# A two-layer encoder trunk: pooling groups and attention heads in turns, two heads projected ahead of the decay, the last norm multiplied early

## The chip, the cores and the metric

The kernel runs on one core of a Trainium2 chip. The metric is the device time of one execution in microseconds; the time before is the median of three runs. Engines are named as the profile names them: TensorE (PE, with its weight loads as PEld), VectorE (DVE), ScalarE (ACT), GpSimd (POOL) and the DMA queue of SyncE (SP).

## The reference

The input x has 512 tokens of 1024 channels in float32. There are two layers, each a token mixer and a feed-forward block, both with a root-mean-square norm ahead of them and a residual behind, and a final norm.

```python
# layer 0: q, k, v and u from one projection of 1024 -> 2048
a_out = diff_attention(q, k, v)      # 4 heads: softmax(q1 k1) - lam * softmax(q2 k2), times v, norm per head
b_out = pool_mixer(u)                # 4 groups of 128 channels: trailing mean over 2, 4, 8, 16 tokens - u, times a 128x128 matrix
x = x + concat(a_out, b_out) @ ab_w_out
x = x + relu(rmsnorm(x) @ w1)**2 @ w2
# layer 1: gated linear attention, 4 heads
q, k, v, g, gk = split(h @ w_in)
log_a = log_sigmoid(gk @ w_gk_up + b_gk) / 16       # the decay, summed up along the tokens of a chunk
o = chunked_linear_attention(q, k, v, log_a)
x = x + (rmsnorm_per_head(o) * silu(g)) @ w_out
x = x + relu(rmsnorm(x) @ w1)**2 @ w2
return rmsnorm(x) * norm_final
```

## The kernel before

Activations lie with the channels on the partitions, 128 at a time, and 512 tokens along the free axis. Every large matmul is done in three passes: weights and activations are each split into a high and a low part (`split_w` at L127 on ScalarE and L128 on VectorE for weights, `split` and `split_scaled` for activations), and high times high, high times low and low times high are added up in PSUM. `proj_T` (L149 to L151) makes one block of 128 output channels: 8 slices of the 1024 inputs, three matmuls each, 24 in all. `proj_tok` (L173 to L175) does the value projections for all four token tiles at once, 96 matmuls on four banks. Weights come in loads of 1 MB (L116) on the SP queue, two blocks a load.

Buffers come from pools with a tag each. The tag `row` has 54 buffers of 512 columns and serves nearly everything (`row`, `row8`, `row16` and `tmp2` are one function; outside the feed-forward blocks every second `tmp` comes from it too). The tag `tmp` has 4, the PSUM tags `mm` (projections) and `ax` (everything else) have 4 banks each. Raw weights and some other stages lie in parts of one large tile (`wraw`), among them a ring of three for the sums of the pooling groups (`row_u`).

The order on each engine is fixed ahead of time by the tile framework's planner. It takes, for each engine, the ready instruction that stands first in the program; `soon(n)`, a high priority, moves an instruction ahead by n places, and `tc.issue_after(i)` holds instructions of an engine behind the instruction i. So TensorE takes later projections when earlier work isn't ready.

Layer 0. The heads' scores and softmax come first (the loop that ends at L392), with the projections of the value and of later stages between. Then `attend(h)` for each of four heads: the value product L372 on TensorE, a square L375, a scaled copy L377, sums over the head (`col_sums`, L203 to L206), a reciprocal root in Ln, Exp and three VectorE steps (L210 to L212), a product L378 and the split L187, L188 into `cat[h]`. The transposes of the last softmax (L354, L356) stand before `attend` of the last head. After all heads come the four pooling groups, windows 16, 8, 4, 2: a projection, its eviction L409, one to four shifted sums L415, the remainder L418 to L421 into a `row` buffer, the product L423 and the split L181, L182 into `cat[4 + i]`. `add_out` then makes the output projection from `cat`; its first two blocks take the slices in order with that of head 3 kept for last (`late`).

Layer 1. Head 0's query and key are projected and evicted (L690, L691), then the decay of all four heads is worked out (L695 to L714: matmul, Abs, Exp, a minimum L700, then Ln under another activation table, a difference L713 and a scan L714). Two calls of `project()` follow in the program (two projections each, evicted by L732 and L735 with `soon()`), and then weights(0), values1(0), weights(1), `project()`, weights(2), values1(1), weights(3), the four `outputs`, the gates and `add_out`. `weights(h)` begins with L747 and L753.

The last feed-forward block works in four quarters c of seven products n each. `gather` (L576) adds a product to the accumulator `acc[t][nh]`: token tile t of four, half nh of two. The last product of the last quarter is done for one token tile after the other, and the final norm follows: squares with their sum (L629), a reciprocal root, and for each half one VectorE step that multiplies by the root and the gain (L637) and a store (L639).

Of the kernel before, what the change touches and what calls it, by code (L numbers as in the profile page):

```python
# [16 lines left out]
P = 128  # L17
S = 512
# [17 lines left out]
def trunk(ctx: ExitStack, tc: tile.TileContext, xT, par, lvl, lam4, wqk0, wu0, wv0, poolw, wo0,  # L36
# [141 lines left out]
    def split_scaled(src, col, tiles=None):  # L178

        ah, al = tiles or act_tiles()  # L180
        A.activation(ah, src, AF.Copy, scale=col)  # L181
        V.scalar_tensor_tensor(out=al, in0=src, scalar=col, in1=ah.bitcast(F32), op0=ALU.mult, op1=ALU.subtract)  # L182
        return ah, al
# [184 lines left out]
    def attend(h):  # L368

        po = PS("ax")  # L370
        for kb in range(NT):
            PE.matmul(po[:, kb * P:], v[kb][:, h * P:(h + 1) * P], pTs[h][kb][:, kb * P:], start=kb == 0,  # L372
                      stop=kb == NT - 1)
        q = tmp()
        A.activation(q, po, AF.Square)  # L375
        o = tmp2()
        A.activation(o, po, AF.Copy, scale=sub8)  # L377
        V.tensor_tensor(o, o, rsqrt(tmp(), col_sums(q, EPS), 1.0 / P), ALU.mult)  # L378
        cat[h] = split(o, (row16(dt=F32R), row16(dt=F32R)))

    pend = []
    for h in range(NH):
# [7 lines left out]
        if h == 1:  # L390
            with tc.issue_after(first_sum):
                values()  # L392
    for h in range(NH - 1):
        attend(h)
    for p in pend:
        transposes(*p)
    attend(NH - 1)


    pw = tmp2().rearrange("p (g c) -> p g c", g=4)  # L400
    nc.sync.dma_start(pw, poolw)
    st = Stream(wu0)
    for i, g in enumerate((3, 2, 1, 0)):
        w = POOL_W[g]
        ps = proj_T(st.next(), act)
        u = row_u()
        G.memset(u[:, 0:16], 0.0)
        with soon():
            V.tensor_tensor(u[:, 16:], ps, rb, ALU.mult)  # L409
        s, step, us = u, 1, [row_u(), row_u()]  # L410
        while step < w:
            s2 = us[0]
            us.reverse()
            G.memset(s2[:, 0:16], 0.0)
            V.tensor_tensor(s2[:, 16:], s[:, 16:], s[:, 16 - step:16 + S - step], ALU.add)  # L415
            s, step = s2, 2 * step
        r = tmp2()
        V.scalar_tensor_tensor(out=r[:, 16:], in0=s[:, 32:], scalar=1.0 / w, in1=u[:, 32:], op0=ALU.mult,  # L418
                               op1=ALU.subtract)
        V.tensor_tensor(r[:, 0:16], s[:, 16:32], prm[:, C_ICNT + 16 * g:C_ICNT + 16 * (g + 1)], ALU.mult)  # L420
        V.tensor_tensor(r[:, 0:16], r[:, 0:16], u[:, 16:32], ALU.subtract)  # L421
        psy = PS("ax")
        PE.matmul(psy, pw[:, g, :], r, start=True, stop=True)  # L423
        cat[NH + i] = split_scaled(psy, prm[:, C_PSC + g:C_PSC + g + 1], (row16(dt=F32R), row16(dt=F32R)))

    def add_out(arr, src, col, late):

# [39 lines left out]
    def ffn(w1, w2, act, nrm, col):  # L467
# [8 lines left out]
        if final:  # L476
            xb = xall.rearrange("p f (t d) -> p f t d", d=P)
            acc = [[xb[:, 4 * nh:4 * nh + 4, t, :] for nh in range(2)] for t in range(NT)]
            gb = [row8() for _ in range(2)]

        def halves():
            return row().rearrange("p (j n) -> p j n", j=2)

        for c in range(4):
# [85 lines left out]
            def gather(t, nh, ps, first=False):  # L570
                with soon():
                    if first and c == 0 and not final:
                        acc[t][nh] = row8()
                        A.activation(acc[t][nh], ps, AF.Copy)
                    else:
                        V.tensor_tensor(acc[t][nh], acc[t][nh], shaped(ps), ALU.add)  # L576

            def shaped(ps):
                return ps.rearrange("p (f d) -> p f d", d=P) if final else ps

            w = [prep(0), prep(1)]
            plan = ((X, True, 0, 0), (Y, True, 0, 0), (X, False, 0, 1), (Zs, True, 2, 1), (X, False, 2, 1),
                    (Zs, False, 0, 1))
            for n, (ps, first, t0, nh) in enumerate(plan):
                if n + 2 < 7:
                    w.append(prep(n + 2))
                product(n, w[n], ps, first)
                for t in range(2):
                    gather(t0 + t, nh, ps[t], n in (0, 2, 3))
            if c == 3 and not final:  # L590
                constants()
            if c < 3:
# [31 lines left out]
                finish(f, pst[f])  # L624
            return nxt, n

        def squares(t, nh, ss):
            q = tmp()
            A.activation(q.rearrange("p (f d) -> p f d", d=P), acc[t][nh], AF.Square, accum_out=ss[:, nh:nh + 1])  # L629

        def finish(t, ss):
            v = small(1)
            V.scalar_tensor_tensor(out=v, in0=ss[:, 0:1], scalar=EPS * D, in1=ss[:, 1:2], op0=ALU.add, op1=ALU.add)
            r = rsqrt(small(1), v, 1.0 / D)
            for nh in range(2):
                o = row8()
                V.scalar_tensor_tensor(out=o.rearrange("p (f d) -> p f d", d=P), in0=acc[t][nh], scalar=r,  # L637
                                       in1=gb[nh].rearrange("p (f d) -> p f d", d=P), op0=ALU.mult, op1=ALU.mult)
                nc.sync.dma_start(out[t * P:(t + 1) * P, nh * S:(nh + 1) * S], o)  # L639

        ss = [small(2) for _ in range(NT)]
        for t in range(2):
            product(6, w[6], X, False, (t,))
            gather(2 + t, 0, X[t])
            if t == 0:
                for u in range(2):
                    squares(u, 0, ss[u])
                    squares(u, 1, ss[u])
                    finish(u, ss[u])
                    squares(2 + u, 1, ss[2 + u])  # L650
            squares(2 + t, 0, ss[2 + t])
            finish(2 + t, ss[2 + t])

    act, nrm = add_out(wo0, cat, C_FFN0, NH - 1)

# [33 lines left out]
    with soon():  # L689
        V.scalar_tensor_tensor(out=qT0, in0=psq0[0], scalar=float(P) ** -0.5, in1=rb, op0=ALU.mult, op1=ALU.mult)  # L690
        evicted = V.tensor_tensor(kT0, psq0[1], rb, ALU.mult).ins  # L691
    es, ms, bs = [], [], []
    for h in range(NH):
        psu = PS("ax")
        PE.matmul(psu, wu[0:96, h * P:(h + 1) * P], gkl[0:96, :], start=True, stop=True)  # L695
        bcol = prm[:, C_BGK + h:C_BGK + h + 1]
        e, m = tmp(), tmp2()
        A.activation(e, psu, AF.Abs, bias=bcol)
        last = A.activation(e, e, AF.Exp, scale=-1.0)
        V.tensor_scalar(out=m, in0=psu, scalar1=bcol, scalar2=0.0, op0=ALU.add, op1=ALU.min)  # L700
        es.append(e)
        ms.append(m)
    with tc.issue_after(last.ins):
        last = A.preload_act_table_set("natural_log")
    with tc.issue_after(last.ins):
# [15 lines left out]
    def expo(out, src):  # L721
        with tc.issue_after(exps):
            last_exp[0] = A.activation(out, src, AF.Exp, scale=GT).ins

    qks = [(qT0, kT0)]

    def project():

        ps = proj_T(st.next(), act)
        qT, kT = row8(), row8()  # L730
        with soon():
            V.scalar_tensor_tensor(out=qT, in0=ps, scalar=float(P) ** -0.5, in1=rb, op0=ALU.mult, op1=ALU.mult)  # L732
        ps = proj_T(st.next(), act)
        with soon():
            V.tensor_tensor(kT, ps, rb, ALU.mult)  # L735
        qks.append((qT, kT))

    def weights(h):

# [119 lines left out]
            ot.append(o)  # L859


    project()
    project()
    weights(0)
    values1(0)
    weights(1)
# [112 lines left out]
```

## Time and profile before

| | us |
|---|---|
| median of three runs | 1107.49 (1107.05 to 1108.73) |
| the profiled execution | 1106.55 |
| its span, first to last instruction | 1104.8 |
| TensorE busy | 1073.0 (97%) |
| VectorE busy | 826.9 (75%) |
| ScalarE busy | 538.3 (49%) |
| mean granted clock of TensorE | 0.990 |

A busy share is that of the span; weight loads overlap the matmuls. The chain of waits that ended last lies on TensorE for 91% of the span, on VectorE for 4% and on ScalarE for 3%. The granted clock is given as a share of 2.4 GHz, so the lower of its two levels, 1.2 GHz, is 0.50.

### The profile page before, as it was taken

The page shows a single profiled execution, that of the slowest core. Times are in us where ns is not written, and L with a number is a line of the kernel's source. Part 1 is how long each engine was busy: PE and PEld are TensorE (multiplying, and loading weights), DVE is VectorE, ACT ScalarE, POOL GpSimd, SP SyncE. Part 2 cuts the span into 40 slices and gives each one's busy share as a digit, 9 for nine tenths or more (in the row PEclk, how much of TensorE's full clock was granted, in tenths as well). Part 3 has the DMA queues.
Part 4 walks back from the last instruction along what each step waited for, and adds up shares of the span by engine and source line. Part 5 has one row for each costly group of instructions (what it writes and reads, how often), then busy time and mean ns, then how long its engine had stood idle before and what let it go on. Part 6 is the DMA issues. An engine that isn't in the chain of part 4 may idle for free.

```text
span 1104.8 us, 12896 instructions
## 1 busy us (share of the span) xinstructions
PE 1073.0 (97%) x4968; PEld 863.6 (78%) x4968; DVE 826.9 (75%) x1234; ACT 538.3 (49%) x890; POOL 2.3 (0%) x20
## 2 busy tenths in 40 slices
PE   7999979999999999999989999999999999999996
PEld 5676648888888888888877778788888888888885
DVE  6847667696497597598878877865696696696696
ACT  6444525455454354454555456844553453453453
POOL 0000000000000000000000000000000000000000
PEclk9999979999999999999999999999999999999999
DMA  6222213214304304203222121433205206206102
GB/s 238 88 89 91 91 72 133 77 39 157 120 28 168 127 11 188 79 17 115 77 77 77 39 77 39 152 114 115 96 1 212 93 1 228 77 3 226 39 1 77
DMA packets 17917, 103.52 MB, mean 94 GB/s; under 512 B 2016, under 2 KB 3040, under 8 KB 6208
## 3 DMA queue, kind: packets, MB, share of 16 engines
q1 hardware_dynamic: 17712, 102.67, 25.8%
q8 instruction: 39, 0.64, 0.2%
q14 instruction: 22, 0.18, 0.1%
q10 hardware_dynamic: 144, 0.03, 0.0%
HBM read 100.59 MB, written 2.10 MB: 93 GB/s over the span
## 4 chain that ended last, share of the span: by engine, by line
PE 91%; DVE 4%; ACT 3%; issue 1%; DMA 1%; SPq 0%; DVEq 0%
PE psmm L149 14%; PE psmm L150 14%; PE psmm L151 14%; PE psmm L568 6%; PE psmm L567 6%; PE psmm L566 6%; PE psax L150 3%; PE psax L151 3%; PE psax L149 3%; PE psax L567 3%; PE psax L568 3%; PE psax L566 3%; PE psmm L173 2%; PE psmm L174 2%; PE psmm L175 2%; PE psax L326 1%
## 5 line engine op out<-in xcount | busy, mean ns | idle before, releaser
L127 ACT ACTIVATE wh<-wraw 128x1024 fp32r<-128x1024 f32 x230 | 243.5, 1061 | 402.6 <-PE psmm L150 161.1
L128 DVE TENSOR_TENSOR wl<-wraw,wh 128x1024 fp32r<-128x1024 f32 x230 | 280.8, 1222 | 70.9 <-ACT wh L127 69.9
L149 PE MATMUL psmm<-row,wh 128*128 128x512 f32 x736 | 289.4, 394 | 15.3 <-DVE wraw L409 7.2
L150 PE MATMUL psmm<-row,wh 128*128 128x512 f32 x736 | 290.7, 395 | 0.0
L151 PE MATMUL psmm<-row,wl 128*128 128x512 f32 x736 | 290.1, 394 | 0.6 <-DVE wl L128 0.6
L149 PEld LDWEIGHTS psmm<-row,wh 128*128 128x128 f32 x736 | 138.5, 189 | 47.8 <-DVE wraw L409 7.8
L151 PEld LDWEIGHTS psmm<-row,wl 128*128 128x128 f32 x736 | 138.8, 189 | 31.9 <-issue 2.6
L150 PEld LDWEIGHTS psmm<-row,wh 128*128 128x128 f32 x736 | 138.8, 189 | 31.0 <-issue 2.6
L566 PE MATMUL psmm<-wh,row 128*128 128x512 f32 x320 | 124.6, 389 | 0.0
L568 PE MATMUL psmm<-wl,row 128*128 128x512 f32 x320 | 124.6, 389 | 0.0
L567 PE MATMUL psmm<-wh,row 128*128 128x512 f32 x320 | 124.5, 389 | 0.0
L541 DVE TENSOR_TENSOR wraw<-wraw 128x1024 f32<-128x1024 f32 x64 | 77.4, 1222 | 0.3
L493 DVE TENSOR_TENSOR row<-row,row 128x512 fp32r<-128x512 f32 x112 | 75.2, 686 | 0.3 <-ACT row L492 0.3
L568 PEld LDWEIGHTS psmm<-wl,row 128*128 128x128 f32 x320 | 60.1, 188 | 12.4
L566 PEld LDWEIGHTS psmm<-wh,row 128*128 128x128 f32 x320 | 60.1, 188 | 12.4
L567 PEld LDWEIGHTS psmm<-wh,row 128*128 128x128 f32 x320 | 60.1, 188 | 12.4
L492 ACT ACTIVATE row<-row 128x512 fp32r<-128x512 f32 x112 | 65.7, 617 | 5.3 <-DVE row L519 5.3
L507 DVE SCALAR_TENSOR_TENSOR tmp<-psmm,rb 128x512 f32<-128x512 f32 x48 | 33.0, 688 | 45.7 <-PE psmm L151 45.7
L512 ACT ACTIVATE row<-tmp 128x256 f32<-128x256 f32 x128 | 45.8, 406 | 11.0 <-DVE tmp L507 10.7
L151 PE MATMUL psax<-row,wl 128*128 128x512 f32 x128 | 49.8, 389 | 0.0
L568 PE MATMUL psax<-wl,row 128*128 128x512 f32 x128 | 49.8, 389 | 0.0
L150 PE MATMUL psax<-row,wh 128*128 128x512 f32 x128 | 49.8, 389 | 0.0
(233 smaller groups left out, 1315.4 us busy)
## 6 DMA issues: line engine op xcount, KB each, us to landing
wraw<-in_w1a SPq DMA_DIRECT2D x16, 1024.0 KB, 4.8
wraw<-in_w2a SPq DMA_DIRECT2D x16, 1024.0 KB, 4.8
wraw<-in_w1b SPq DMA_DIRECT2D x16, 1024.0 KB, 4.8
wraw<-in_w2b SPq DMA_DIRECT2D x16, 1024.0 KB, 4.8
wraw<-in_wo SPq DMA_DIRECT2D x8, 1024.0 KB, 4.8
wraw<-in_wqk SPq DMA_DIRECT2D x7, 1024.0 KB, 4.8
wraw<-in_wv SPq DMA_DIRECT2D x6, 1024.0 KB, 4.7
wraw<-in_wg SPq DMA_DIRECT2D x4, 1024.0 KB, 4.8
```

Of the source, the lines that this page charges most:

```text
L127: ended["hi"] = A.activation(hi, src, AF.Copy).ins
L128: ended["lo"] = V.tensor_tensor(lo, src, hi.bitcast(F32), ALU.subtract).ins
L149: PE.matmul(ps, wh, ah, start=first, stop=False)
L150: PE.matmul(ps, wh, al, start=False, stop=False)
L151: ended["mm"] = PE.matmul(ps, wl, ah, start=False, stop=last).ins
L492: A.activation(hi, src, AF.Copy)
L493: V.tensor_tensor(lo, src, hi.bitcast(F32), ALU.subtract)
L512: A.activation(raw[name][:, j, :], r[:, th * 256:th * 256 + 256], AF.Square)
L541: V.tensor_tensor(out[k], in0[k], in1[k], ALU.subtract)
L566: PE.matmul(ps[t], hi, wh[:, cs], start=f, stop=False, skip_group_check=True)
L567: PE.matmul(ps[t], lo, wh[:, cs], start=False, stop=False, skip_group_check=True)
L568: PE.matmul(ps[t], hi, wl[:, cs], start=False, stop=l, skip_group_check=True)
```

## The change

Three edits. First, the loop over pooling groups becomes a function `pooled(i, g)`, and the program calls pooled(0), attend(0), pooled(1), attend(1), pooled(2), attend(2), the last transposes, pooled(3), attend(3). The load of the pooling matrices stays ahead of all of it. Second, `project()` and its first two calls move ahead of the decay, and the decay's first loop is put under `soon(150)`. Third, in the last quarter of the last feed-forward block, when products 1 and 4 are gathered, two quarters of the output are final: `early` takes their squares and multiplies them with the gain at once (`zs`). In the tail `finish(t)` then does one VectorE step for the other half, and ScalarE scales the early half by the root in place; both are stored. The order of the tail changes: the gather of token tile 2 comes ahead of the finish of tiles 0 and 1.

```diff
-    for h in range(NH - 1):
-        attend(h)
-    for p in pend:
-        transposes(*p)
-    attend(NH - 1)
...
-    for i, g in enumerate((3, 2, 1, 0)):
+
+    def pooled(i, g):
...
+    for h in range(NH - 1):
+        pooled(h, 3 - h)
+        attend(h)
+    for p in pend:
+        transposes(*p)
+    pooled(3, 0)
+    attend(NH - 1)
...
+            ss, zs = [small(2) for _ in range(NT)], {}
...
+            def squares(t, nh):
+                q = tmp()
+                A.activation(blocks(q), acc[t][nh], AF.Square, accum_out=ss[t][:, nh:nh + 1])
+
+            def early(t, nh):
+
+                squares(t, nh)
+                zs[t] = row8()
+                V.tensor_tensor(blocks(zs[t]), acc[t][nh], blocks(gb[nh]), ALU.mult)
...
                     gather(t0 + t, nh, ps[t], n in (0, 2, 3))
+                    if final and c == 3 and n in (1, 4):
+                        early(t0 + t, nh)
...
-            for nh in range(2):
-                o = row8()
-                V.scalar_tensor_tensor(out=o.rearrange("p (f d) -> p f d", d=P), in0=acc[t][nh], scalar=r,
-                                       in1=gb[nh].rearrange("p (f d) -> p f d", d=P), op0=ALU.mult, op1=ALU.mult)
-                nc.sync.dma_start(out[t * P:(t + 1) * P, nh * S:(nh + 1) * S], o)
...
+            nh = 1 if t < 2 else 0
+            o = row8()
+            V.scalar_tensor_tensor(out=blocks(o), in0=acc[t][nh], scalar=r, in1=blocks(gb[nh]), op0=ALU.mult,
+                                   op1=ALU.mult)
+            nc.sync.dma_start(out[t * P:(t + 1) * P, nh * S:(nh + 1) * S], o)
+            A.activation(zs[t], zs[t], AF.Copy, scale=r)
+            nc.sync.dma_start(out[t * P:(t + 1) * P, (1 - nh) * S:(2 - nh) * S], zs[t])
+
+        product(6, w[6], X, False, (0,))
+        gather(2, 0, X[0])
         for t in range(2):
...
+            squares(t, 1)
+            finish(t)
+        product(6, w[6], X, False, (1,))
+        squares(2, 0)
+        finish(2)
+        with soon():
+            gather(3, 0, X[1])
+            squares(3, 0)
+            finish(3)
...
+    qks = [(qT0, kT0)]
+
+    def project():
+
+        ps = proj_T(st.next(), act)
+        qT, kT = row8(), row8()
+        with soon():
+            V.scalar_tensor_tensor(out=qT, in0=ps, scalar=float(P) ** -0.5, in1=rb, op0=ALU.mult, op1=ALU.mult)
+        ps = proj_T(st.next(), act)
+        with soon():
+            V.tensor_tensor(kT, ps, rb, ALU.mult)
+        qks.append((qT, kT))
+
+    project()
+    project()
     es, ms, bs = [], [], []
     for h in range(NH):
...
+        with soon(150):
+            psu = PS("ax")
...
-    project()
-    project()
     weights(0)
```

## Rows read from the trace of the kernel before

**Rows 1.** Waits of TensorE: engine, line, releaser, us, times, longest.
```profile
PE psmm L149 <- DVE wraw L409: 7.2, 1, 7.2
```

**Rows 2.** GLA stage in order of time: start us, us, engine, line, operation, tiles.
```profile
546.35 0.39 PE L151 MATMUL psmm<-row,wl 128*128 128x512 f32 x1
...
556.73 0.63 ACT L699 ACTIVATE row<-row 128x512 f32<-128x512 f32 x1
...
565.12 2.33 DVE L714 TENSOR_TENSOR_SCAN row<-row,row 128x512 f32<-128x512 f32 x2
567.37 0.67 DVE L732 SCALAR_TENSOR_TENSOR row<-psmm,rb 128x512 f32<-128x512 f32 x1
...
568.09 0.80 PE L173 MATMUL psmm<-wh,row 128*128 128x512 f32 x1 [2.95 <-DVE row L732]
...
570.94 0.68 DVE L753 TENSOR_TENSOR tmp<-row 128x512 f32<-128x512 f32 x1
...
619.79 0.68 DVE L732 SCALAR_TENSOR_TENSOR row<-psmm,rb 128x512 f32<-128x512 f32 x1
```

**Rows 3.** Stretches: length, busy PE, PEld, DVE, ACT, POOL, then PEclk, DMA, GB/s.
```profile
134.80:148.15 13.35, 3.46 (x8) 1.61 (x8) 7.77 (x14) 4.34 (x8) 0.00 (x0) 0.61 0.48 177
148.15:151.40 3.25, 3.25 (x5) 1.50 (x5) 2.06 (x3) 0.69 (x1) 0.44 (x4) 0.52 0.00 0
568.10:571.20 3.10, 3.10 (x8) 2.50 (x9) 3.10 (x6) 0.00 (x0) 0.00 (x0) 0.51 0.00 0
668.80:721.70 52.90, 51.56 (x281) 43.54 (x280) 42.25 (x67) 40.84 (x57) 0.00 (x0) 1.00 0.29 100
1060.00:1087.00 27.00, 27.00 (x121) 22.37 (x120) 23.67 (x30) 14.28 (x18) 0.00 (x0) 1.00 0.00 1
```

**Rows 4.** The tail in order of time.
```profile
1087.35 0.69 DVE L576 TENSOR_TENSOR x<-x,psax 128x512 f32<-128x512 f32 x1 [0.26 <-PE psax L568]
...
1090.08 0.75 DVE L637 SCALAR_TENSOR_TENSOR row<-x,sm,row 128x512 f32<-128x512 f32 x1
...
1095.08 0.39 PE L568 MATMUL psmm<-wl,row 128*128 128x512 f32 x1
...
1096.00 0.68 DVE L576 TENSOR_TENSOR x<-x,psmm 128x512 f32<-128x512 f32 x1
...
1099.55 1.41 DVE L637 SCALAR_TENSOR_TENSOR row<-x,sm,row 128x512 f32<-128x512 f32 x2
1100.33 1.09 SPq L639 DMA_DIRECT2D out<-row  x2
```

**Rows 5.** Heads and pooling groups in order of time.
```profile
109.38 2.32 PE L372 MATMUL psax<-row,wraw 128*128 128x512 f32 x8
111.73 0.60 ACT L375 ACTIVATE tmp<-psax 128x512 f32<-128x512 f32 x1 [0.74 <-PE psax L372]
111.97 0.75 DVE L347 SCALAR_TENSOR_TENSOR wraw<-wraw,sm 128x512 f32<-128x512 f32 x1
...
119.96 0.69 DVE L188 TENSOR_TENSOR row<-row,row 128x512 fp32r<-128x512 f32 x1 [0.70 <-ACT row L187]
...
145.79 0.69 DVE L188 TENSOR_TENSOR row<-row,row 128x512 fp32r<-128x512 f32 x1 [0.69 <-ACT row L187]
146.40 0.67 DVE L418 SCALAR_TENSOR_TENSOR row<-wraw 128x496 f32<-128x496 f32 x1
...
147.40 0.69 DVE L409 TENSOR_TENSOR wraw<-psmm,rb 128x512 f32<-128x512 f32 x1
...
153.15 1.07 PE L423 MATMUL psax<-row,row 128*128 128x512 f32 x2
```

**Rows 6.** Costliest groups of the page: xcount, busy us, mean ns, idle before.
```profile
L128 DVE TENSOR_TENSOR wl<-wraw,wh 128x1024 fp32r<-128x1024 f32 x230 | 280.8, 1222 | 70.9 <-ACT wh L127 69.9
```

**Rows 7.** Groups of TensorE from 104.9 to 165.7.
```profile
L151 PE MATMUL psmm<-row,wl 128*128 128x512 f32 x44 | 18.4, 422 | 0.0
```

**Rows 8.** Groups of TensorE from 568 to 595.
```profile
L173 PE MATMUL psmm<-wh,row 128*128 128x512 f32 x26 | 11.3, 434 | 3.0 <-DVE row L732 3.0
```

More of the change, by code (lines that the diff above doesn't have):

```diff
@@ L575, in gather, with blocks @@
                     else:
-                        V.tensor_tensor(acc[t][nh], acc[t][nh], shaped(ps), ALU.add)
-            def shaped(ps):
+                        V.tensor_tensor(acc[t][nh], acc[t][nh], blocks(ps), ALU.add)
+            def blocks(ps):
                 return ps.rearrange("p (f d) -> p f d", d=P) if final else ps
+            def squares(t, nh):
[5 more added lines that the diff above has]
+                V.tensor_tensor(blocks(zs[t]), acc[t][nh], blocks(gb[nh]), ALU.mult)
             w = [prep(0), prep(1)]
@@ L625, in ffn, with finish @@
             return nxt, n
[L627 to L631, printed above, removed]
+        def finish(t):
             v = small(1)
-            V.scalar_tensor_tensor(out=v, in0=ss[:, 0:1], scalar=EPS * D, in1=ss[:, 1:2], op0=ALU.add, op1=ALU.add)
+            V.scalar_tensor_tensor(out=v, in0=ss[t][:, 0:1], scalar=EPS * D, in1=ss[t][:, 1:2], op0=ALU.add, op1=ALU.add)
             r = rsqrt(small(1), v, 1.0 / D)
-            for nh in range(2):
-                o = row8()
-                V.scalar_tensor_tensor(out=o.rearrange("p (f d) -> p f d", d=P), in0=acc[t][nh], scalar=r,
-                                       in1=gb[nh].rearrange("p (f d) -> p f d", d=P), op0=ALU.mult, op1=ALU.mult)
-                nc.sync.dma_start(out[t * P:(t + 1) * P, nh * S:(nh + 1) * S], o)
-        ss = [small(2) for _ in range(NT)]
-        for t in range(2):
[L643 to L652, printed above, removed]
+            nh = 1 if t < 2 else 0
[7 more added lines that the diff above has]
+        gather(2, 0, X[0])
+        for t in range(2):
+            squares(t, 1)
[7 more added lines that the diff above has]
+            finish(3)
     act, nrm = add_out(wo0, cat, C_FFN0, NH - 1)
@@ L691, in trunk @@
         evicted = V.tensor_tensor(kT0, psq0[1], rb, ALU.mult).ins
+    qks = [(qT0, kT0)]
[10 more added lines that the diff above has]
+    project()
     es, ms, bs = [], [], []
     for h in range(NH):
[L694 to L702, printed above, removed]
+        with soon(150):
+            psu = PS("ax")
+            PE.matmul(psu, wu[0:96, h * P:(h + 1) * P], gkl[0:96, :], start=True, stop=True)
+            bcol = prm[:, C_BGK + h:C_BGK + h + 1]
+            e, m = tmp(), tmp2()
+            A.activation(e, psu, AF.Abs, bias=bcol)
+            last = A.activation(e, e, AF.Exp, scale=-1.0)
+            V.tensor_scalar(out=m, in0=psu, scalar1=bcol, scalar2=0.0, op0=ALU.add, op1=ALU.min)
+            es.append(e)
+            ms.append(m)
     with tc.issue_after(last.ins):
@@ L723, in expo @@
             last_exp[0] = A.activation(out, src, AF.Exp, scale=GT).ins
[L725 to L736, printed above, removed]
     def weights(h):
```

## The prediction

> **What bounds the kernel now.** I read the waits of TensorE first, then the stretches around them, then the order on VectorE inside each. TensorE is the bound almost everywhere and nearly never waits. Two of its waits concern this change: one on L409, in the first layer between attention and output projection [rows 1], and one on L732, in the GLA stage [rows 2]. In the first, from 134.80 to 148.15, TensorE is busy 3.46 of 13.35 us, at a mean granted clock of 0.61, and the 3.25 us after it still run at 0.52 [rows 3]. Counted against full clock that loses 9.9 + 1.35 + 1.55 = 12.8 us. The second wait loses 2.95 us (565.14 to 568.09 [rows 2]) and, at a clock of 0.51 for the 3.1 us after it [rows 3], 1.5 more: 4.4 us. The third place is the tail: the last matmul ends at 1095.47, the program 9.3 us later [rows 4].
>
> **Why they wait.** The reader should see what stands directly ahead of the late instruction. L732 evicts a projection that TensorE finished at 546.74; it runs at 567.37, right behind the last scans L714, although it is marked urgent [rows 2]. The next L732 comes only at 619.79, when the second head of the weights is through. L418, the pooling remainder, runs at 146.40, right behind the split L188 of the last attention head [rows 5]. Each writes a fresh buffer of the pool `row`, and comes right behind the instruction that, in the program, takes the buffer of that pool just before it. I infer that the planner hands out the buffers of one pool in the order in which the program first writes them, whether or not there are free ones, and work this through the new order.
>
> **Pooling and heads in turns.** Nothing is removed: four projections, the same DMAs, the same arithmetic. The pooling weights' DMA keeps its place on SP behind the same load, now issued before it is needed. Today all four heads run first, then the four pooling groups. Afterwards head 0's buffers come behind group 0's, group 1's behind head 0's last split, and so on, so that one chain runs through all eight. The prices [rows 5]: group 0's L418 can start when the softmax ends, 112.7. A remainder is 1.0 (146.40 to 147.40), its product half of the 1.07 of the L423 pair (0.5), the head's value product 2.35 (109.38 to 111.73), from its square L375 to the split L188 8.23 (111.73 to 119.96), and the next L418 stands 0.6 behind a split. That is 12.7 us for a group and a head, against 8.6 for a head alone today ((145.79 - 119.96) / 3). The last split ends at 112.7 + 4 x 12.7 = 163.5 at the earliest. Projection work hides only the first turn: the three remaining pooling projections are 72 matmuls of 0.223 (27.00 us hold 121 [rows 3]), 16 us from 105 on, used up at about 126 with the first turn between; after that TensorE has the chain's own matmuls (0.5 + 2.1 + 0.4 for the sums, 3 us per turn) and, queued behind each group's product, one slice of each open output block at a time. In such a stretch today the clock stands at 0.61 [rows 3]. At half clock a turn's 3.0 us of matmuls cost 3.0 more, for one turn wholly and for another half: 4.5, so 168. The planner also puts weight splits (1.2 us each) and the sums of the next group between the chain's VectorE steps [rows 6]; I take 2 us: 170.
>
> The Trainium skill ("TensorE: Matmul & The Clock Gate", Part 1) has the idle array throttled by default, with activity releasing it; the trace agrees with 0.61 and 0.52 around today's wait, and by that rule the middle turns would be slow as well. Without the low clock the sum would be 4.5 less.
>
> To compare: before its last split the new order can do 24 slices of the pooling projections and 20 of the output projection (two blocks of 7, two of 3, as four PSUM banks allow), 44 of each of the three lines. Today the 44th L151 stands at 165.7 [rows 7]. So this part costs 170 - 165.7 = +4.3; bounds -2.2 (163.5) and +11.6 (every later turn at half clock, 9.0, and a split in each, 4.8: 177.3).
>
> **Two heads projected ahead of the decay.** The four evictions now come as each projection ends, so the 4.4 us go. But the decay's buffers now stand behind the last of these evictions. Today the decay runs under the projections. Now its L700 can't start before the fourth projection is evicted (ends 565.1, eviction 0.6). Two of the four heads' Abs and Exp take such buffers too: three of these at 0.63 stand before the last Exp, and from that to the end of the last scan it is 10.7 us (556.73 to 567.45) [rows 2]. So the end is at 565.7 + 1.9 + 10.7 = 578.3, and the first L753 at 579 against 570.94, 8 us late (6.5, if steps overlap, to 9.5, with a weight split more between). Behind L700 on VectorE stand only weight splits, which are marked urgent and planned ahead of it, so TensorE goes on; the value projection (96 matmuls, 21 us) covers these 8 us. What is late next: the third head pair's evictions (L732 at 619.8, now about 627.8) wait for head 1's buffers, and until then only 96 + 48 + 48 = 192 projection matmuls can run, as two of the four banks are held. A head takes about 25 us and uses 77 of them (26 of each of three lines in 27 us that hold a head and a little more [rows 8]); the first 14 us use 63: 63 + 77 + 77 = 217, so 25 are missing and TensorE stands about 5.5 us. In all: from 619.8 to 721.7 there are 100.6 us of TensorE work today (1.3 idle [rows 3]); of it 192 - 78 - 77 = 37 matmuls, 8.3 us, are then done, leaving 92.3 from 627.8, plus 1 for the clock: 721.1, against 721.7. With those 1.3 idle kept the part is worth about 0; bounds -4.4 (cover throughout) and +4 (the outputs' chain, 8 us later, ends after the gates).
>
> **Last norm.** Four squares and four products with the gain (0.68 each, 2.7 us) move into the last feed-forward quarter, where VectorE is busy 23.67 of 27 us and TensorE 27 [rows 3]: the 3.3 us free there take them; without that cover up to 2.7 us of stall. In the tail each token tile then has one L637 instead of two; ScalarE scales the other half (0.6) beside it. Today the last gather L576 starts at 1096.00, half a us after the last matmul, held by two L637; the final pair runs 1099.55 to 1100.96 and its second store is issued last [rows 4]. Undisturbed, L576 to L637 takes 2.73 (1087.35 to 1090.08): with the gather at 1095.5 to 1096.2 and one L637 of 0.75 the end is 1099.0 to 1099.7, but the two stores now become ready together and one is issued 0.55 behind the other (1.09 for two). I take -1.1; bounds -1.9 and +1.6.
>
> **Sum.** 4.3 + 0 - 1.1 = +3.2 us. The profiled execution took 1106.55 (span 1104.8), so 1109.7 for its like; its median stands 0.94 higher, 1107.49, so 1110.7. The measurement tells about 0.2%, 2.2 us, from no change.
>
> **Rivals.** Just covered: the first part costs 1 (few splits collide), GLA gives 0.5, the tail 1.1: 1106.9, no change. Clock kept: if the sparse matmuls hold the clock at 2.4 GHz and no split collides, the chain ends at 163.5 (-2.2), GLA gives 2.2 (L753 only 6.5 late), the tail 1.1: -5.5, 1102.0. It decides if the clock row between 127 and 154 stays near 1.00; the 0.61 speaks against it. No such order: if a pool's buffers are free for whoever is ready, both stalls fill with projections: -12.8 - 4.4 - 1.1 = -18.3, 1089.2. Three late evictions speak against it. The Trainium skill ("Perfetto Trace Analysis", Optimization Strategy) advises to interleave regimes with different limits, which is this case. Late outputs: the decay comes 9.5 us late, the outputs' chain ends after the gates and TensorE stands there: GLA +4, in all 1114.7; today's 1.3 us of idle TensorE in that stretch [rows 3] are its first sign, the gates still left then speak against it.
>
> **How the numbers follow.** Forecast 0.40 (own range 1109.7 to 1114); just covered 0.27; clock kept 0.15; no such order 0.09; late outputs 0.09. Faster 0.24, same 0.27, slower 0.49. The range leaves out "no such order" and the far end of the slow cases: 1101.5 to 1115.5.
>
> **What would show it.** Right: L418 of group 1 directly behind head 0's L188, near 125, the four L418 about 13 to 16 us apart, the last split near 170, low clock between 130 and 155; L700 behind L735 near 565, L753 near 579, TensorE idle shortly before 628; one L637 in the tail. Wrong: L418 four times before 135, or TensorE full from 127 to 160; L700 before 560; weight splits late in the last quarter because of the early products.

## The result, and the profile after

The changed kernel takes 1101.02 us (median of four, 1100.49 to 1101.40) against 1107.29 on the same chip: a ratio of 0.9942, with a 95% interval of 0.9930 to 0.9954, or 6.4 us less. Forecast were 1110.7 and a range from 1101.5 to 1115.5. The time lies half a microsecond below that range, on the other side of the kernel before. Of the ten runs of delay16, one of the experiments below, two were far slower (1202.93 and 3804.46 us) and are left out of its median.

Three marks in the two traces say which edit moved what. The GLA stage begins with the eviction of the decay's input, L685 at 546.2 before and L700 at 546.7 after. The last matmul ends at 1095.47 before and 1091.04 after (1090.65 + 0.39). The spans end at 1104.8 and 1098.7.

| edit | its marks | forecast | traces |
|---|---|---|---|
| pooling and heads in turns | start of the GLA stage | +4.3 | +0.5 |
| two heads projected ahead | from there to the last matmul's end: 549.2, then 544.3 | 0 | -4.9 |
| last norm | from there to the end of the span: 9.3, then 7.7 | -1.1 | -1.7 |

Two of these marks carry less than their digits. The stage begins at 546.9 in b_only and at 547.2 in c_only, two of the experiments, whose first layer is that of the kernel before; so +0.5 lies within what an unchanged first layer varies. And the unchanged tail takes 8.5 us rather than 9.3 in a_only and b_only; against those the last norm's -1.7 is -0.8.

Line numbers have moved: the remainder L418 is now L413, the pooling eviction L409 is L404, the evictions L732 and L735 are L714 and L717, the decay's minimum (L700 before) is L731 and its scan L745, L753 is L771, the gather L576 is L581, L637 is L650, and the stores are L652 and L654.

First the wait of TensorE that answers to [rows 1], in the view of the waits from 100 to 175 (engine, line, releaser; us in all, times, longest).

```profile
PE psmm L149 <- ACT row L187: 9.0, 2, 4.9
```

The one wait of 7.2 us on the pooling eviction, with 2.1 on a head's split, has become two waits on heads' splits, 9.0 us in all. The stall was not removed but moved. VectorE's order shows why; it answers to [rows 5].

```profile
111.38 0.67 DVE L413 SCALAR_TENSOR_TENSOR row<-wraw 128x496 f32<-128x496 f32 x1
...
121.16 0.69 DVE L211 SCALAR_TENSOR_TENSOR tmp<-tmp,row 128x512 f32<-128x512 f32 x1
121.83 1.23 DVE L128 TENSOR_TENSOR wl<-wraw,wh 128x1024 fp32r<-128x1024 f32 x1
122.97 0.68 DVE L212 SCALAR_TENSOR_TENSOR row<-tmp,row 128x512 f32<-128x512 f32 x1
...
125.08 0.69 DVE L188 TENSOR_TENSOR row<-row,row 128x512 fp32r<-128x512 f32 x1 [0.70 <-ACT row L187]
125.69 0.67 DVE L413 SCALAR_TENSOR_TENSOR row<-wraw 128x496 f32<-128x496 f32 x1
...
137.89 0.69 DVE L188 TENSOR_TENSOR row<-row,row 128x512 fp32r<-128x512 f32 x1 [0.69 <-ACT row L187]
138.50 0.67 DVE L413 SCALAR_TENSOR_TENSOR row<-wraw 128x496 f32<-128x496 f32 x1
...
151.87 0.69 DVE L188 TENSOR_TENSOR row<-row,row 128x512 fp32r<-128x512 f32 x1 [0.69 <-ACT row L187]
152.47 0.67 DVE L413 SCALAR_TENSOR_TENSOR row<-wraw 128x496 f32<-128x496 f32 x1
...
165.68 0.69 DVE L188 TENSOR_TENSOR row<-row,row 128x512 fp32r<-128x512 f32 x1 [0.70 <-ACT row L187]
```

Each remainder stands directly behind the split of the head before it, as the prediction had it. The turns take 14.3, 12.8, 14.0 and 13.9 us, the fourth counted to the end of its split. The last split starts at 165.68 and ends at 166.37, 0.7 behind the break-even of 165.7 [rows 7]. The stretches of the two waits, in the columns of [rows 3]:

```profile
132.95:137.91 4.96, 0.05 (x1) 0.00 (x0) 2.78 (x5) 1.85 (x3) 0.00 (x0) 0.70 0.00 0
137.91:141.39 3.48, 3.48 (x5) 1.63 (x6) 2.91 (x6) 0.00 (x0) 0.00 (x0) 0.50 0.00 0
147.80:151.89 4.09, 0.04 (x2) 0.01 (x1) 2.79 (x5) 1.15 (x3) 0.00 (x0) 1.00 0.65 248
151.89:155.36 3.47, 3.46 (x5) 1.54 (x6) 1.51 (x4) 0.11 (x1) 0.00 (x0) 0.51 0.00 0
```

Two idle stretches of 4.96 and 4.09 us are each followed by 3.5 us at the lower clock, which cost 1.7 us each: 9.0 + 3.4 = 12.4 us lost, against 12.8 before.

In the GLA stage the order on VectorE answers to [rows 2].

```profile
565.05 0.69 DVE L717 TENSOR_TENSOR row<-psmm,rb 128x512 f32<-128x512 f32 x1 [3.35 <-PE psmm L151]
565.65 0.74 DVE L731 TENSOR_SCALAR row<-psax,par 128x512 f32<-128x512 f32 x1
...
574.98 2.33 DVE L745 TENSOR_TENSOR_SCAN row<-row,row 128x512 f32<-128x512 f32 x2
577.23 0.66 DVE L771 TENSOR_TENSOR tmp<-row 128x512 f32<-128x512 f32 x1
...
598.45 0.68 DVE L771 TENSOR_TENSOR row<-row 128x512 f32<-128x512 f32 x1
...
621.08 0.68 DVE L714 SCALAR_TENSOR_TENSOR row<-psmm,rb 128x512 f32<-128x512 f32 x1
```

The decay's minimum L731 stands right behind the last eviction L717, and the first step of the weights comes at 577.23: forecast were 565.7 and 579. But the third pair's eviction comes at 621.08, not at 627.8. TensorE over the whole stage, before (first fence) and after:

```profile
546.00:722.00 176.00, 171.48 (x1011) 136.33 (x1010) 141.56 (x263) 104.78 (x172) 0.00 (x0) 0.99 0.21 72
```

```profile
622.00:672.00 50.00, 50.00 (x343) 40.03 (x342) 41.59 (x90) 27.20 (x51) 0.00 (x0) 1.00 0.18 64
672.00:722.00 50.00, 48.45 (x253) 40.15 (x252) 42.14 (x66) 41.19 (x57) 0.00 (x0) 1.00 0.27 96
546.00:722.00 176.00, 173.94 (x1033) 140.01 (x1032) 143.31 (x265) 107.97 (x175) 0.00 (x0) 1.00 0.21 76
```

In the same 176 us TensorE now does 22 more matmuls, at 0.223 us 4.9 us of work. It is full from 622 to 672; the 1.55 us idle near the end of the stage were 1.34 before.

The tail, to be held against [rows 4]:

```profile
1090.65 0.39 PE L573 MATMUL psmm<-wl,row 128*128 128x512 f32 x1
...
1091.58 0.68 DVE L581 TENSOR_TENSOR x<-x,psmm 128x512 f32<-128x512 f32 x1
...
1094.31 0.72 ACT L653 ACTIVATE row<-row,sm 128x512 f32<-128x512 f32 x1 [0.61 <-DVE sm L212]
1094.31 0.75 DVE L650 SCALAR_TENSOR_TENSOR row<-x,sm,row 128x512 f32<-128x512 f32 x1
1095.06 0.33 SPq L654 DMA_DIRECT2D out<-row  x1
1095.49 0.38 SPq L652 DMA_DIRECT2D out<-row  x1
```

The last gather still starts half a microsecond after the last matmul, but L650 now begins 2.73 us behind it, 3.55 before, and there is one of them. The last store is issued 4.83 us after the last matmul (1095.87 - 1091.04), 5.95 before (1100.33 + 1.09 - 1095.47): 1.1 us, as forecast. The other half microsecond is the time from that issue to the end of the span, 2.8 against 3.4. The edit needn't have given it: in a_only, which has the old tail, that time is 2.65 (last issue ends at 1103.46, the span at 1106.11).

### The profile page after: what moved, and what is told of

It is laid out like the page before. It is cut to its first block, busy times and chain, and to the rows that moved or that the text cites. A ratio compares the mean times of both kernels' runs of the same rounds, so it can differ in the third digit from the quotient of the medians.

```text
span 1098.7 us, 12896 instructions
## 1 busy us (share of the span) xinstructions
PE 1071.5 (98%) x4968; PEld 863.5 (79%) x4968; DVE 825.5 (75%) x1234; ACT 540.9 (49%) x894; POOL 2.3 (0%) x20
## 4 chain that ended last, share of the span: by engine, by line
PE 90%; ACT 4%; DVE 4%; issue 1%; DMA 1%; SPq 0%; DVEq 0%; ACTq 0%
PE psmm L150 14%; PE psmm L149 14%; PE psmm L151 14%; PE psmm L571 6%; PE psmm L572 6%; PE psmm L573 6%; PE psax L151 3%; PE psax L149 3%; PE psax L150 3%; PE psax L573 2%; PE psax L571 2%; PE psax L572 2%; PE psmm L174 2%; PE psmm L173 2%; PE psmm L175 2%; PE psax L326 1%
## 5 line engine op out<-in xcount | busy, mean ns | idle before, releaser
L151 PEld LDWEIGHTS psmm<-row,wl 128*128 128x128 f32 x736 | 138.9, 189 | 30.5 <-issue 1.1
L571 PEld LDWEIGHTS psmm<-wh,row 128*128 128x128 f32 x320 | 60.1, 188 | 12.4
L149 PE MATMUL psax<-row,wh 128*128 128x512 f32 x128 | 49.8, 389 | 0.0
L150 PE MATMUL psax<-row,wh 128*128 128x512 f32 x128 | 49.8, 389 | 0.0
```

Of the source, the lines that this page charges most:

```text
L149: PE.matmul(ps, wh, ah, start=first, stop=False)
L150: PE.matmul(ps, wh, al, start=False, stop=False)
L151: ended["mm"] = PE.matmul(ps, wl, ah, start=False, stop=last).ins
L571: PE.matmul(ps[t], hi, wh[:, cs], start=f, stop=False, skip_group_check=True)
```

## Experiments

**Each edit alone.** Kernel before, with one of the three edits of the diff above and nothing of the others.

a_only:

```diff
+    for h in range(NH - 1):
+        pooled(h, 3 - h)
+        attend(h)
...
+    pooled(3, 0)
+    attend(NH - 1)
```

> Only the first edit: pooling groups and heads in turns; decay and tail as in the kernel before. My reading of the changed kernel's trace: the chain of turns ends at 165.7, where the kernel before had done the same number of output-projection matmuls, and the GLA stage starts 0.5 us later than before. So 1107.3 + 0.5 = 1107.8 us (1106.8 to 1108.8). Rival 1, the prediction's own size (turns at 13.5 us on average, low clock in one and a half turns): 1111.6. Rival 2, that the turns gained and the decay only seemed to: 1103 or less.

b_only:

```diff
+    project()
+    project()
     es, ms, bs = [], [], []
...
-    project()
-    project()
     weights(0)
```

> Only the second edit: two heads projected ahead of the decay. My reading: the wait of 2.95 us and the low clock behind it go (4.4 us) and nothing takes their place, because a head of the weights takes 21 to 23 us rather than 25 and the third head's evictions come at about 620.5 in this kernel, just before the projections run out: 1107.3 - 5.0 = 1102.3 us (1101.5 to 1103.0). Rival, the prediction's step: the projections run out before the evictions and TensorE stands about 5.5 us before 628: 1107. In the trace no TensorE wait over 0.5 us between 546 and 625 by my reading, one of 3 us or more by the rival.

c_only:

```diff
+                    if final and c == 3 and n in (1, 4):
+                        early(t0 + t, nh)
...
+            A.activation(zs[t], zs[t], AF.Copy, scale=r)
```

> Only the third edit: the last norm's early products. The tail from the end of the last matmul to the end of the span was 9.3 us before and 7.7 us in the changed kernel: 1107.3 - 1.6 = 1105.7 us (1105.2 to 1106.2), with the last matmul where it was. Rival, the prediction's size (the second store of the last tile costs half a us): 1106.2; that early products stall the last quarter: 1106.5 or more and a later last matmul.

Measured against 1107.49: a_only 1106.58, ratio 0.9992 (0.9983 to 1.0001); b_only 1101.36, 0.9944 (0.9931 to 0.9956); c_only 1106.83, 0.9994 (0.9986 to 1.0003). All three lie outside the ranges noted for them, b_only by 0.1 and a_only by 0.2 us on the fast side, c_only by 0.6 on the slow side. b_only also shows the prediction's step missing by itself. That step wanted a wait of TensorE of 3 us or more before 628; from 546 to 625 the longest in b_only is

```profile
PE psax L761 <- DVE tmp L758: 0.3, 1, 0.3
```

So the second edit alone is nearly the whole gain, the turns are worth nothing that can be told, and the last norm is too small for this test. The three sum to 7.7 us, the whole change gave 6.4; the intervals, of about 1 us each, cover that. The single runs of a_only spread from 1105.6 to 1108.2. Its profiled execution took 1107.92, and its last split shows part of that:

```profile
152.83 0.69 DVE L188 TENSOR_TENSOR row<-row,row 128x512 fp32r<-128x512 f32 x1 [0.69 <-ACT row L187]
...
167.13 0.69 DVE L188 TENSOR_TENSOR row<-row,row 128x512 fp32r<-128x512 f32 x1 [0.70 <-ACT row L187]
```

The same chain took 1.45 us more here than in the trace above (167.13 against 165.68), after two turns equal to 0.02 us.

**The pool's order.** All three edits, and four buffers of their own for the remainders:

```diff
-        return T([P, n], "row", 54, dt)
+        return T([P, n], "row", 50, dt)
...
-        r = tmp2()
+        r = T([P, S], "pl", 4)
```

> All three edits, and the pooling remainders get four buffers of their own, taken from the pool `row` (50 left of 54). If buffers are handed out in program order within a pool, the remainder no longer has to stand behind the split of the head before: the second remainder moves from 125.7 to about 115, groups overlap with heads, the heads follow each other at 8.6 to 10 us as in the kernel before, the last split comes near 150 rather than 165.7 and most of the 12.6 us that TensorE still loses there (9.2 idle, 3.4 low clock) goes: 1101.0 - 9 = 1092 us (1089 to 1096). Rival: the order comes from elsewhere (the planner's taste for program order, the ring of the sums, the PSUM banks): remainders stay behind the splits, 1101 +- 1. A loss would mean that the pool `row` needs its 54 buffers.

1088.28 us (1087.89 to 1088.46; 1089 to 1096 was expected), ratio to before 0.9825 (0.9811 to 0.9838): 12.7 us below the changed kernel, for two lines that change no arithmetic. The remainders in this kernel, and the stretch around them in it (second fence) and in the changed kernel (third):

```profile
111.62 0.67 DVE L413 SCALAR_TENSOR_TENSOR pl<-wraw 128x496 f32<-128x496 f32 x1
...
118.23 0.68 DVE L413 SCALAR_TENSOR_TENSOR pl<-wraw 128x496 f32<-128x496 f32 x1
...
126.87 0.69 DVE L188 TENSOR_TENSOR row<-row,row 128x512 fp32r<-128x512 f32 x1
...
133.23 0.67 DVE L413 SCALAR_TENSOR_TENSOR pl<-wraw 128x496 f32<-128x496 f32 x1
```

```profile
127.00:155.00 28.00, 26.34 (x108) 18.76 (x107) 19.23 (x32) 12.99 (x25) 0.11 (x1) 1.00 0.33 113
```

```profile
127.00:155.00 28.00, 18.80 (x56) 10.73 (x56) 15.69 (x26) 9.26 (x19) 0.22 (x2) 0.82 0.20 75
```

The second remainder comes 8.6 us before the first head's split instead of right behind it. TensorE does 108 matmuls in these 28 us instead of 56, at full clock. So it was the pool's order that tied the remainders to the heads, not the program's order, the ring of the sums or the PSUM banks, none of which changed. That 50 buffers are left of 54 can't be what helped. Nor were buffers short: with 44 in place of 54 and nothing else (row44, below) the second to fourth remainders again start 0.61 us behind the split of the head before.

**What the turns are worth without that tie.** The same, with the first edit undone (all heads, then all groups):

> Second and third edit and own buffers for the pooling remainders, but the first edit undone: all heads, then all groups. It tells what the turns are worth once the pool's order no longer ties the remainders to the heads. My reading: the turns still place the groups' products and splits early, so their slices of the output projection can fill TensorE while the heads run; without them the four products (PSUM banks are handed out in program order too) come behind the last head, near 146, and TensorE runs dry from about 138 to 147: 1094 to 1098. Rival: own buffers alone do it, the turns add nothing: 1088.3 as with both.

1094.29 us (1093.92 to 1094.76); the same stretch of its trace:

```profile
127.00:155.00 28.00, 22.16 (x81) 14.69 (x79) 16.20 (x26) 12.24 (x23) 0.00 (x0) 0.94 0.35 122
```

As expected: the turns give 6.0 us once the remainders are free, and nothing before. The Trainium skill ("Perfetto Trace Analysis", Optimization Strategy) says that performance may be improved by interleaving stretches in which different engines are the most contended; these two kernels agree with it, a_only doesn't.

**How late may the decay come?** The changed kernel with idle steps in the decay (eight, then sixteen):

```diff
             V.tensor_tensor(m, m, e, ALU.subtract)
+            for _ in range(2):     # 4 in delay16
+                V.tensor_scalar(out=m, in0=m, scalar1=1.0, scalar2=None, op0=ALU.mult)
```

> The changed kernel with eight idle VectorE steps (two multiplications by 1.0 in place for each head, 0.6 us each, 4.8 us) between the decay's differences and scans, so the first step of the weights comes at about 582 rather than 577.2. My reading: of the 192 projection matmuls that TensorE may run before the third pair of queries and keys is evicted, the changed kernel uses 182, so 10 (2.3 us) are left; with the evictions 4.8 us later TensorE stands about 2.5 us shortly before 626, and the low clock behind it costs up to 1.5 more: 1101.0 + 2.5 to 4 = 1103.5 to 1105. Rival: nothing runs dry in this stage at any lateness: 1101.0, no wait. Second rival: every microsecond of lateness is paid at the end of the stage: 1105.8.

> The same with sixteen idle steps (9.6 us), the weights from about 587. My reading: TensorE stands 7 to 7.5 us before 631, then a low clock: 1101.0 + 7.3 to 9 = 1108.3 to 1110, so the slope between the two delays is about 1 us per us, after a first 2.3 us that are free. Rival, nothing runs dry: 1101.0. Second rival, paid at the end: 1110.6, with TensorE idle near 720 and not before 631.

1102.73 and 1106.11 us, 1.7 and 5.1 above the changed kernel. The weights begin 33.2 and 35.9 us after the stage's first eviction (580.72 and 584.01, from 547.5 and 548.1), against 30.5 in the changed kernel: only 2.7 and 5.4 us later, as part of the steps ran beside ScalarE. My reading was wrong in its place. TensorE waits for no more than 0.5 us before the third pair's evictions in either kernel, though these come 3.5 and 5.0 us later by the same mark. delay16 pays at the end of the stage instead; the waits and the stretch from 672 to 722:

```profile
PE psax L205 <- ACT row L203: 2.0, 1, 2.0
PE psax L867 <- DVE wraw L855: 0.8, 1, 0.8
```

```profile
672.00:722.00 50.00, 47.08 (x254) 39.89 (x253) 38.00 (x63) 36.71 (x51) 0.00 (x0) 0.97 0.25 85
```

L205 sums over a head's output, L867 belongs to the outputs, and 2.9 us of idle time and a clock of 0.97 stand there, where the changed kernel has 1.55 and 1.00. From the stage's first eviction to the end of the last matmul it is 544.33 us in the changed kernel, 545.79 with eight steps and 548.73 with sixteen: of 2.7 us of lateness 1.5 are paid, of 5.4 us 4.4. So the first 1.0 to 1.2 us are free, and the changed kernel's own lateness has that much to spare. The second rival, paid at the end, holds for most of the 4.4 us (1.4 of idle time and 1.5 of clock in the stretch above); where the rest is lost isn't shown, nor for eight steps, whose idle time in the 190 us from the first eviction is 2.3 us against 2.1.

**An early decay.** The decay's buffers in a pool of their own:

```diff
-            e, m = tmp(), tmp2()
+            e, m = T([P, S], "dc", 10), T([P, S], "dc", 10)
...
-        b = row16()
+        b = T([P, S], "dc", 10)
```

> The changed kernel, in which the decay's Abs, minimum and scan results get ten buffers of their own, taken from the pool `row` (44 left). If the pool's order is what put the decay behind the last eviction, its first minimum moves from 565.65 to before 555 and the first step of the weights from 577.2 to about 571 as in the kernel before; if the order comes from the program or the planner, both stay. The time: by my reading lateness of 6 us is covered, so 1101.0 less what the stage's end gives back (TensorE idles 1.55 us from 672 to 722): 1099.5 to 1101.3. Rival, that the covered lateness still costs low clock or VectorE time somewhere: 1098 or less.

1103.30 us (1102.88 to 1105.03), 2.3 above the changed kernel. The order moved as the pool's order says: the first minimum stands at 553.35, the weights begin at 570.65. But the time rose, which neither theory had. The trace (a minimum on VectorE, then TensorE's one new long wait):

```profile
553.35 0.75 DVE L731 TENSOR_SCALAR dc<-psax,par 128x512 f32<-128x512 f32 x1 [2.28 <-ACT dc L729]
...
572.78 0.55 PE L776 MATMUL psax<-par,tmp 128*128 128x128 f32 x3 [1.67 <-DVE tmp L773]
```

In the changed kernel the same wait is 0.3 us. The transposes L776 of the first head's weights stand in TensorE's order ahead of further projections, and wait 1.67 us for L773. Did the early start cost the time, or the ten buffers taken from `row`? Two more kernels tell: the changed kernel with 44 buffers and nothing else, and the kernel before, with the evictions of project() in own buffers, so that its gap goes but the decay stays early:

```diff
-        qT, kT = row8(), row8()
+        qT, kT = T([P, S], "qk", 6), T([P, S], "qk", 6)
```

> The changed kernel with nothing but the pool `row` cut from 54 to 44 buffers. It is the control for the early decay and the groups' own splits, which both ran with 44. If buffers are never short at 44: 1101.0 (1100.4 to 1101.7), and the 2.3 and 1.4 us lost there belong to the new order. If 44 are too few: 1102 to 1103.5, and those losses say nothing on the order.

> The kernel before, with six own buffers for the queries and keys that project() evicts (48 left in `row`) and nothing else: the gap of 4.4 us goes without the decay being put late. It tells what made the first head take 25.5 us. If that was the gap and the low clock at its head: the first head takes 21 to 23 us here too, TensorE is full, and the time is 1107.3 - 4.9 = 1102.4 (1101.7 to 1103.1), as with the second edit. If an early start of the weights makes the first head slow by itself, as with the decay in own buffers (23.5 us and a wait of 1.7 us on the transposes): the first head takes 23.5 us or more and the time is 1104 to 1105.

row44 takes 1102.20 us (1101.54 to 1102.64), ratio to before 0.9949 (0.9935 to 0.9962), which overlaps the changed kernel's 0.9942 (0.9930 to 0.9954). It lies in the range that I gave for too few buffers, but the trace puts that elsewhere: the last split of the turns starts at 167.14, as in a_only, and the GLA stage didn't change. From the stage's first eviction to the last matmul's end it takes 544.35 us (548.82 to 1093.17), as the changed kernel's 544.33; with the early decay it is 546.48 (546.75 to 1093.23). So the early decay costs 2.1 us, and the 44 buffers nothing in that stretch.

qk_own takes 1104.51 (1103.11 to 1107.53), ratio 0.9977 (0.9968 to 0.9986): 3.1 us less by the medians, 2.5 by the ratio, of the 4.9. Its eleven runs fall in two groups, six from 1103.11 to 1104.51 and five from 1106.04 to 1107.53, and the trace is of the run at 1106.04. The two first steps of its weights, TensorE's wait between them, and TensorE behind that wait and from 570 to 622:

```profile
570.96 0.66 DVE L753 TENSOR_TENSOR tmp<-row 128x512 f32<-128x512 f32 x1
...
596.50 0.68 DVE L753 TENSOR_TENSOR row<-row 128x512 f32<-128x512 f32 x1
```

```profile
573.18 0.72 PE L758 MATMUL psax<-par,tmp 128*128 128x128 f32 x3 [1.97 <-DVE tmp L755]
```

```profile
573.55:577.00 3.45, 3.45 (x11) 2.71 (x10) 2.58 (x5) 1.01 (x2) 0.00 (x0) 0.53 0.13 55
570.00:622.00 52.00, 50.03 (x319) 38.69 (x318) 42.53 (x90) 25.67 (x49) 0.00 (x0) 0.97 0.19 66
```

The first head takes 25.5 us with the gap gone, but this doesn't clear the gap. Here the head holds a wait of its own, 1.97 us, and 3.45 us at a clock of 0.53 behind it, which cost 1.6 more. In the early decay it takes 23.55 us (570.65 to 594.20) with 1.67 us of waiting. Less that both heads come to about 22 us, against 21.2 in the changed kernel and 22.9 and 23.2 with the delays, which hold waits of 0.3 to 0.5. In the kernel before TensorE is busy in the whole of the first head, at full clock; why that head takes 25.5 isn't shown.

What an early start costs is shown by the marks. From the stage's first eviction to the last matmul's end it is 549.24 us in the kernel before, 546.48 with the gap gone and an early decay, 544.33 with the gap gone and a late one: 2.8 us for the gap, 2.1 for the early start. qk_own's trace has 548.04 (547.11 to 1095.15), that is 546.4 without its 1.6 of low clock.

**On the best kernel.** With own buffers for the remainders the single runs of a kernel lie within 1.1 us, so small edits can be sized. The reference again, the reference without the third edit, with the groups' splits in own buffers too, with the decay in own buffers, and with 44 buffers in `row`:

> The three edits and own buffers for the pooling remainders once more, as the reference of the next kernels on the same chip: 1088.3 (1087.7 to 1088.8), a spread of some 0.6 us, since no stretch is left in which the clock falls.

> As the reference, but without the third edit (the early products of the last norm). Alone it gave 0.7 +- 1 us in runs that spread over 2.4 us; here the spread is small enough to size it. My reading of the tails: the last store is issued 5.95 us after the last matmul ends in the kernel before and 4.83 to 5.12 with the edit: 1088.3 + 1.0 = 1089.3 us (1089.0 to 1089.8). Rival, that the span's end counts (9.3 against 7.7): 1089.9 or more. Rival, that it gives nothing: 1088.3.

> As the reference, but the groups' splits into the concatenation get own buffers too (ten in all, 44 left in `row`), so that nothing of the groups stands in the heads' order but the PSUM banks. If the remainder was the only tie that mattered: 1088.3 +- 0.4. If the splits hold the heads back too (in the reference the heads are 7.7 to 10.1 us apart against 8.6 in the kernel before): 1086.5 to 1087.5.

> As the reference, with the decay's buffers taken out of the pool's order as well (ten buffers shared by the remainders and the decay). On the changed kernel that cost 2.3 us, of which 1.7 was one wait of TensorE for the transposes of the first head's weights. If that wait belongs to the early decay, it is here again: 1090.0 to 1090.8. If it was an accident of that order of instructions: 1087 to 1088.5.

> The three edits, four own buffers for the remainders, and `row` cut to 44 rather than 50: the same control on the best kernel. Buffers never short: 1088.2 +- 0.4. Too few: 1089.4 to 1091, as with own buffers for the groups' splits and for the decay.

1088.07 (1087.70 to 1088.44), 1088.46 (1088.35 to 1088.87), 1089.44 (1089.11 to 1089.58), 1090.91 (1090.24 to 1091.11) and 1088.55 us (1088.31 to 1089.34). The last norm's edit is worth 0.4 us by the medians, less than the 1.0 expected and less than either kernel's runs spread (0.7 and 0.5), though the last VectorE step of the tail ends 1.46 us nearer to the last matmul: 1081.52 + 0.75, with the matmul's end at 1078.23, against 1082.22 + 1.41 and 1078.13 without the edit.

```profile
1081.52 0.75 DVE L650 SCALAR_TENSOR_TENSOR row<-x,sm,row 128x512 f32<-128x512 f32 x1
```

```profile
1082.22 1.41 DVE L640 SCALAR_TENSOR_TENSOR row<-x,sm,row 128x512 f32<-128x512 f32 x2
```

Part of that is given back as forecast: two stores are ready at once and one is issued behind the other. More freedom for the groups' splits lost 1.4 us, a miss on the other side; 44 buffers alone cost 0.5 of it, and the cause of the rest is open. The early decay lost 2.8, 2.4 of it beyond the kernel with 44 buffers, with the same wait of 1.7 us on L776 in its trace: that wait belongs to the early decay. By the marks above it takes 546.49 us from the stage's first eviction to the last matmul's end (534.30 to 1080.79), the kernel with 44 buffers 544.36 (534.47 to 1078.83), again 2.1 apart.

## Why the prediction was wrong, step by step

**The order.** Right, and it carried everything else. Both places it foretold (a remainder behind each head's split, the minimum behind the last eviction) are in the trace within 1 us of the forecast, and own buffers undid both. The rival "no such order" gave 1089.2 for this change. The changed kernel isn't that case, but the kernel in which the order is broken for the remainders takes 1088.3.

**Pooling and heads in turns: +4.3 forecast, +0.5 in the trace, 0.9 less +- 1.0 alone.** The mechanism was right and the size off. Of the 6.5 us that I put on top of the earliest end, 163.5, only 2.9 came (166.37). The start gave 1.3 back (111.38, not 112.7), and the four turns together ran 4.2 over their 4 x 12.7 = 50.8. Of these 1.6 lie in the first turn, at full clock: there a weight split of 1.23 us stands between L211 and L212, which start 1.81 us apart and 0.72 in the second turn. The third and fourth turns have 1.3 and 1.2; at the head of each stands a spell of half clock that cost TensorE 1.7, not a turn and a half throughout. So the terms that were too large are the clock (4.5) and the collisions (2). I had read 0.61 and 0.52 [rows 3] as the state of a sparse stretch. In the trace after, the clock is 1.00 from 144 to 152 with TensorE busy 3.95 of 8 us; its work runs at half clock only in the 3.5 us behind each of the two idle spells. The Trainium skill ("TensorE: Matmul & The Clock Gate", Part 1) has the idle array throttled by default, with activity releasing it; the trace agrees, with 0.50 behind 4.96 idle us and 0.51 behind 4.09, though in the second of these idle spells itself the granted clock still reads 1.00.

**Two heads ahead: 0 forecast, -4.9 in the traces and -6.1 (4.9 to 7.6) alone.** This is the step that failed: that TensorE would run out of projections and stand about 5.5 us shortly before 628. The 4.4 us went as forecast, and the weights started late as forecast (577.23; forecast 579). But nothing ran dry: TensorE is full from 622 to 672, and b_only, with this edit alone, has no wait over 0.3 us before 625. I took "a head takes about 25 us" from the kernel before (570.94 to 596.49, and 596.49 to 621.7 for the second) and put it in twice. From the first step of the weights to the third pair's eviction it is 48.9 us there, 48.8 in the forecast and 43.9 in the changed kernel (21.2 for the first head, 22.6 from there to the eviction). So the evictions came at 621, and by then TensorE had run 182 matmuls of the 192 I allowed, not the 217 I counted on. The 25.5 us were no property of a head: VectorE was busy in 20.30 of them and in 19.64 of the 21.2. Why the heads are shorter behind a late start was not settled. Nor is lateness as such a cost: an early decay is 2.1 us dearer in two kernels (decay_own, rd_own), of which the wait at the transposes is 1.4 (1.7 against 0.3); the rest is open. The rival "late outputs" named the place where most of it is paid in delay16, but by the delays lateness is paid only from about 1 us beyond where the change puts it.

**Last norm: -1.1 forecast.** The traces show 1.7, of which 1.1 lies before the last store's issue and was forecast; the rest is a span's end that the old tail also reaches. The best pair of kernels shows 0.4. The last quarter hid the early products: TensorE waits for nothing there.

**The sum** came out 9.7 us too high: 3.8 from the turns, 4.9 from the heads, 0.6 from the tail, and 0.4 because the median stands 0.53 above the profiled execution here (1100.49), not 0.94. The rival that came nearest was "clock kept", 1102.0, and it was near by luck. Its turns came 2.7 us worse than it said (+0.5, not -2.2) and its GLA stage 2.7 better (-4.9, not -2.2), and the clock was not kept: it is 0.84 from 127 to 154.

## What to carry to other kernels

Where one pool serves everything, its order is a hidden chain through the program: when an urgent instruction runs directly behind an unrelated one, look for the pool that both take a fresh buffer from, and give the one that is to run ahead a few buffers of its own. Here two lines gave 12.7 us, twice what the reordering gave, and made the reordering worth its 6. And a stage's length read at one place in a schedule is no fixed price: two heads took 25.5 and 25.2 us in the kernel before, and the first takes 21.2 after. The busy time of the engine that its steps run on (20.3 us of VectorE) says how short it may get, and belongs in the range. Being early can cost, too: here 2.1 us.

## What the runs showed of the hardware

In the changed kernel TensorE's work ran at a granted clock of 0.50 and 0.51 for 3.5 us behind idle spells of 4.96 and 4.09 us, which cost 1.7 us each. Shorter spells had the same behind them: 2.95 us in the kernel before (0.51 for 3.1 us) and a wait of 1.97 us in qk_own (0.53 for 3.45 us). Behind the wait of 1.67 us in decay_own the clock stayed at 1.00. Whether such spells make times spread isn't shown: the eleven runs of a_only lie within 2.6 us of each other, but the four of the changed kernel, with the same two waits in the first layer, within 0.9, and those of each kernel with own buffers for the remainders and the turns within 1.1.
